# Bias rows at a pitch of 2 KB, longer assumed transfers in the list scheduler, and a new layout of the first transfers and products

## The chip, the core and the metric

The kernel runs on one core of one Trainium2 chip. The engines named here are TensorE (PE, its weight loads PEld), VectorE (DVE), ScalarE (ACT), GpSimd (POOL) and SyncE (SP, which issues nearly all transfers). The metric is the device time in microseconds (us), and less is better.

## What is computed

Two layers of an encoder over 768 tokens (512 of one request, 256 of another) with 1024 features, in float32. Layer 0 mixes tokens by windowed attention, layer 1 by a short convolution. The change lies in layer 0's mixer and in what is loaded for it:

```python
bias = rel_bias[t5_bucket(rel)]                      # 16 heads, 128 x 384 per query block
q, k, v = split(rms_norm(x, norm_mix[0]) @ w_qkv)    # 16 query heads, 4 key heads of 64
logits = q @ k.T * scale + bias, masked to +-128 tokens
p = softmax(logits with the sink)                    # out = p @ v, x = x + out @ w_o
...
x = x + (p[i] @ ple_w_proj[i]) * gate                # the product p[i] @ ple_w_proj[i] comes first
```

Every float32 operand of a product is split into a high and a low part (`hi`, `lo`), and three products stand for one: hi by hi, lo by hi, hi by lo.

## The kernel before

`mixer_attention` writes layer 0's mixer as a list of operations with costs. `Plan.order` is a list scheduler: it walks through them in a modelled time, engine by engine, and takes at each point the ready operation with the longest way to the end (`reach`). The order that comes out is what each engine's queue holds, in order. The modelled time of a transfer is its `lands` (bytes by 400 GB/s) behind a common pipe, 1.7 us after the issue, and 0.3 us more until it counts as landed (`done`, L549 and L550). The engines themselves run by semaphores, so the model only sets the order. SP, ACT and DVE each take their own queue strictly in order: an entry that waits holds up all entries behind it.

In that part of the program:

- **First products.** `p0` (two blocks of 128x768) and `w0` (128x1024) are loaded, split (L782 to L796), and multiplied for eight blocks m of 128 output rows, each in two pieces of 512 and 256 columns (`product`, L664, `halves`); `projected` copies the results to tiles `L` and stores them (`pj`). Ahead of them, PE runs matmuls on constants (`dummy`, tile `warm`, L755) and one product for the bias rows (`bp`, L762).
- **Inputs.** x is loaded in eight blocks (`x_in`), scaled and split to `xs` (L834, L837); squares are summed (L846, L848) for the norm, whose `rstd` reaches DVE late, at L878. Products by `w_k` and `w_q` need all of `xs`; their scaling (`kt`, `qt`) needs `rstd`.
- **Bias rows.** `brow` holds for each of 16 heads one row of 512 numbers. One transfer writes each row 32 times into DRAM (`skew`) with a pitch of SKEW numbers; 32 later transfers (`bias<-skew`, four to a tile, 16 to the first two head groups together) read it at a pitch of SKEW-1, so that each query's row is shifted by one.
- **Heads.** The halves of `kt` and `qt` that hold single heads are copied between partitions by transfers (`kk<-qh`, `kk<-ql`, `q<-qh`, `q<-ql`, 64 partitions each). Scores (`S`, L1052 and L1053) need q and k; the reduction behind them (L1059) needs the bias.
- **Values.** `values(n)` (`vp`, L980 to L982) multiplies xs by the three pieces of `w_v` (`wvh`, `wvl`); ACT and DVE empty its bank into `vv` (L995, L998). Tiles `wraw` are a ring of three buffers for loaded weights; a bank of PSUM with the tag mm1 exists once.

The layer's input p[1] is loaded to `wraw` and split within the same stage (`p`, L1180, L1183). After the attention stage the kernel leaves this scheduler; from there on its order is written out by hand.

Of the kernel before, what the change touches and what calls it, by code (L numbers as in the profile page):

```python
# [17 lines left out]
P = 128  # L18
# [9 lines left out]
CH = 1024  # L28

BM, BS, BO, BT, BL = 1, 3, 1, 2, 5  # L30

NA = 2
URGENT = 10.0

# [4 lines left out]

SKEW = 511  # L40
ROWS = 32
# [6 lines left out]
def trunk_kernel(ctx: ExitStack, tc: tile.TileContext, a: dict, out: bass.AP):  # L48
# [423 lines left out]
    class Plan:  # L472


        OWN = {"PE": 0.0, "ACT": 0.13, "DVE": 0.12, "POOL": 0.1, "SP": 0.0}
        OTHER = {"PE": 0.22, "ACT": 0.15, "DVE": 0.14, "POOL": 0.3, "SP": 0.1}
# [86 lines left out]
    def mixer_attention():  # L563
# [46 lines left out]
        def place(i, name, dt=F32R):  # L610
            return new(f"S{i}", 1, lambda: slot(i, name, dt))

        def dma(box, src, n, after=(), uses=(), queue="SP"):

            def run():
                d, s = src()
                (nc.sync if queue == "SP" else act).dma_start(d, s)

            lands = n / 400e3
# [33 lines left out]

        def product(ps, w, xs, o, n, col=0, ks=None, start=True, stop=True, prev=None):

            ks = range(len(xs)) if ks is None else ks
            for i, k in enumerate(ks):

                def run(i=i, k=k):
                    c = slice(col, col + P)  # L660
                    wh, wl = w.parts[0][k][:, c], w.parts[1][k][:, c]
                    xh, xl = (p[:, o : o + n] for p in xs[k].parts())
                    for j, (a_, b_) in enumerate(((wh, xh), (wh, xl), (wl, xh))):
                        pe.matmul(  # L664
                            ps.t[:, :n],
                            lhsT=a_,
                            rhs=b_,
                            start=start and i == 0 and j == 0,
                            stop=stop and i == len(ks) - 1 and j == 2,
                        )  # L670

                args = "PE", 3 * MM[n], run, [w.ready, xs[k].ready, prev], [ps.key, *w.keys, *xs[k].keys]
                if i == 0 and start:
                    prev = first(ps, *args[:3], args[3], args[4][1:])
                else:
                    prev = op(*args)
            return prev

        def halves(w, xs, tags, col=0):

            o, out = 0, []
            for tag, n in zip(tags, SEQS):
                ps = bank(tag)
                out.append((ps, o, n, product(ps, w, xs, o, n, col)))
                o += n
            return out
# [26 lines left out]
        def widen():  # L713
# [20 lines left out]
        table = op("ACT", 1.28, lambda: act.preload_act_table_set(EXP_LN), behind=[mk_in])  # L734
        got[1] = [dma(p0[1], lambda: (p0[1].t[:], a["p"][0, :, 1, :]), 393216)]
        w0.landed.append(
            dma(w0, lambda: (w0.t[:, 512:], a["proj"][0, 0, :, 512:]), 262144, uses=[w0.key])
        )
        w1 = fetched(a["proj"][0, 1])
        vec_in = dma(None, lambda: (vec[:], a["vec"][:]), 40960)  # L740
        x_in = []
        for m in range(KB):
# [3 lines left out]
            x_in.append(dma(b, lambda b=b, m=m: (b.t[:, m % 2, :], a["x"][m]), 393216, uses=[] if m % 2 == 0 else [b.key]))  # L746
        wk = fetched(a["w_k"][0])
        sink_in = dma(None, lambda: (sink[:], a["sink"][:].broadcast_to([P, HEADS])), 8192)
        for u, v in zip(DMAS := [got[0][0], w0.landed[0], got[1][0], w0.landed[1], w1.landed[0], vec_in, *x_in, wk.landed[0], sink_in], DMAS[1:]):
            v.behind.append(u)  # L750

        def dummy(n):
# [4 lines left out]

        d0 = first(warm, "PE", 3 * 0.45, dummy(3), [wide], [ones512.key])
        bp = bank("PT", "bp")
        bps = first(  # L760
            bp, "PE", 1.0,
            lambda: pe.matmul(bp.t[:HEADS, :], lhsT=rb.t[:], rhs=oh.t[:], start=True, stop=True),  # L762
            [rb_in, oh_in, d0], [rb.key, oh.key],
        )
# [10 lines left out]
        wt.keys, wt.ready = [wt.key], []  # L775
        part0 = []
        for k in range(2):
            c = slice(512 * k, 512 * k + 512)
            hi, lo = place(10 + k, "p0h"), place(12 + k, "p0l")

            def wh(c=c, k=k):
                act.activation(wt.t[0][:, c], w0.t[:, c], AF.Copy)  # L782
                wt.parts = [blocks(t[:], 2) for t in wt.t]

            def wl(c=c):
                dve.tensor_tensor(wt.t[1][:, c], w0.t[:, c], wt.t[0][:, c].bitcast(F32), ALU.subtract)

            if k == 0:
                h = first(wt, "ACT", A(512), wh, [w0.landed[0]], [w0.key])
                ph = first(hi, "DVE", 0.5, lambda hi=hi: dve.tensor_copy(hi.t[:], p0[0].t[:]), [got[0]], [p0[0].key])  # L790
            else:
                h = op("ACT", A(512), wh, [w0.landed[1]], [wt.key, w0.key])
                ph = first(hi, "ACT", A(T), lambda hi=hi: act.activation(hi.t[:], p0[1].t[:], AF.Copy), [got[1]], [p0[1].key])
# [4 lines left out]
            )  # L798
            l = op("DVE", V(512), wl, [h], [wt.key, w0.key])
            part0.append(block_of(hi, lo, [ph, pl, h, l]))  # L800
        w1 = prepared(w1, 2)
# [6 lines left out]
        def projected(l, m, w, part, t, tags, vector):  # L808
            ops = []
            for ps, o, n, last in halves(w, part, tags, m % 4 * P):  # L810

# [68 lines left out]
        rc = new("rc", 1, lambda: ap.tile([P, T // P], F32, name="rc", bufs=1))  # L880
        rt = bank("O", "rt")

# [3 lines left out]

        tr = first(rt, "PE", 0.4, columns, [rstd, d1], [r.key])
        rcs = first(rc, "DVE", 0.1, lambda: dve.tensor_copy(rc.t[:], rt.t[:, : T // P]), [tr], [rt.key])
# [22 lines left out]
        def keys(c, ps, tag):  # L911
            parts = scaled(ps, temp(tag, "kt"), False, tag)
            for j in range(2):
                g = 2 * c + j
                for kept, places, (part, ready) in ((khh, KHI, parts[0]), (kll, KLO, parts[1])):
                    dst = kept[g] = place(places[g], "kk")
                    dst.ready = []
                    for i in range(2):
# [6 lines left out]

                        dst.ready.append(dma(dst, ends, 196608, [ready], [part.key] + ([dst.key] if i else [])))

        def queries(c, w, tags, tag):
            parts = scaled(halves(w, xs, tags), temp(tag, "qt"), True, tag)
            for j in range(2):  # L930
# [3 lines left out]
                for i, (part, ready) in enumerate(parts):  # L934
# [6 lines left out]

                    dst.ready.append(dma(dst, ends, 196608, [ready], [part.key] + ([dst.key] if i else [])))

# [6 lines left out]
            ),  # L950
            1046528 * 4, [rowed], [brow.key],
        )
# [50 lines left out]
        for n in range(T // P):  # L1003
            values(n, ("O", "mm1")[n % 2] if n < 3 else "mm1")

# [1046 lines left out]
```

## Time and profile before

| | us |
|---|---|
| three runs, median (lowest, highest) | 1678.84 (1677.44, 1679.71) |
| the profiled execution, its own time | 1679.09 |
| its span in the trace | 1677.3 |

The page's second part cuts the span into 40 slices, with the busy share of each engine in tenths and the clock granted to TensorE (`PEclk`). A view by windows gives the same sums for stretches that one chooses. A view of waits names, for an engine, the instruction that stood idle and the last thing that released it. In a timeline a row holds start, duration, engine, line, operation, output and inputs, and in brackets the idle time ahead of it with its releaser. `SPq` rows are issues of transfers.

### The profile page before, as it was taken

How to read it: one execution, taken by the hardware profiler on the slowest of the kernel's cores; microseconds unless marked ns; L12 is line 12 of the kernel's file. 1: busy time of each engine (PE TensorE's matmuls, PEld its weight loads, DVE VectorE, ACT ScalarE, POOL GpSimd, SP SyncE). 2: the span in 40 equal slices, each digit the busy share in tenths (PEclk: the TensorE clock that was granted, in tenths of full speed). 3: DMA queues.
4: the chain of work that ended last, by engine and by line, in shares of the span. 5: the costliest groups of instructions: out<-in, count | busy, mean ns of one | idle time of the engine just before them, and what ended most of it. 6: DMA issues, size and time to landing. Idle time of an engine off the chain costs nothing. (4 is left out here: it accounts for less than half of the span.)

```text
span 1677.3 us, 24258 instructions
## 1 busy us (share of the span) xinstructions
PE 1641.3 (98%) x9428; PEld 1594.0 (95%) x9428; DVE 1394.3 (83%) x2215; ACT 919.9 (55%) x1454; POOL 13.5 (1%) x60
## 2 busy tenths in 40 slices
PE   9899899999999999999999999999999999999996
PEld 7788788999999999999999999999999999999986
DVE  6368598999899899886878877759989989998676
ACT  6269586765555555554655334545555545554554
POOL 0000000000000000000000000000000000000000
PEclk9899899999999999999999999999999999999998
DMA  9644432212222222122321221211122222222222
GB/s 265 165 113 139 107 95 91 97 50 72 76 73 67 76 76 76 64 95 66 111 82 51 76 76 63 89 63 51 64 76 76 70 69 76 76 67 85 79 89 98
DMA packets 47843, 144.59 MB, mean 86 GB/s; under 512 B 6080, under 2 KB 10688, under 8 KB 47728
## 3 DMA queue, kind: packets, MB, share of 16 engines
q1 hardware_dynamic: 47600, 142.94, 27.3%
q8 instruction: 74, 1.21, 0.3%
q14 instruction: 41, 0.34, 0.1%
q10 hardware_dynamic: 128, 0.10, 0.0%
HBM read 123.10 MB, written 10.48 MB: 80 GB/s over the span
## 5 line engine op out<-in xcount | busy, mean ns | idle before, releaser
L429 ACT ACTIVATE whi<-sum 128x1024 fp32r<-128x1024 f32 x66 | 70.1, 1062 | 257.8 <-PE a L461 221.8
L461 PE MATMUL a<-xs,whi 128*128 128x384 f32 x608 | 118.0, 335 | 0.7 <-DVE y L1549 0.6
L461 PEld LDWEIGHTS a<-xs,whi 128*128 128x128 f32 x608 | 106.4, 188 | 1.6 <-DVE y L1549 1.3
L461 PE MATMUL a<-t,whi 128*128 128x384 f32 x528 | 107.6, 336 | 0.0
L461 PE MATMUL b<-t,zhi 128*128 128x384 f32 x528 | 107.6, 336 | 0.0
L461 PE MATMUL a<-t,zhi 128*128 128x384 f32 x528 | 107.2, 336 | 0.0
L1585 DVE TENSOR_TENSOR x<-x,a 128x384 f32<-128x384 f32 x112 | 62.1, 554 | 53.7 <-PE a L461 53.6
L461 PE MATMUL a<-act,whi 128*128 128x384 f32 x448 | 96.1, 335 | 0.0
L461 PEld LDWEIGHTS a<-t,whi 128*128 128x128 f32 x528 | 93.4, 188 | 0.0
L461 PEld LDWEIGHTS b<-t,zhi 128*128 128x128 f32 x528 | 93.4, 188 | 0.0
L461 PEld LDWEIGHTS a<-t,zhi 128*128 128x128 f32 x528 | 93.3, 188 | 0.0
L429 ACT ACTIVATE zhi<-sum 128x1024 fp32r<-128x1024 f32 x66 | 69.8, 1057 | 36.9 <-DVE sum L405 31.2
L440 DVE TENSOR_TENSOR wlo<-wraw,whi 128x1024 fp32r<-128x1024 f32 x72 | 87.6, 1217 | 0.0
L429 ACT ACTIVATE whi<-wraw 128x1024 fp32r<-128x1024 f32 x72 | 75.6, 1050 | 19.4 <-issue 15.8
L664 PE MATMUL mm<-xs_mix,whi 128*128 128x512 f32 (+1 forms) x320 | 84.8, 354 | 0.2 <-ACT L L817 0.2
L440 DVE TENSOR_TENSOR zlo<-sum,zhi 128x1024 fp32r<-128x1024 f32 x66 | 80.4, 1218 | 0.5 <-ACT zhi L429 0.5
L440 DVE TENSOR_TENSOR wlo<-sum,whi 128x1024 fp32r<-128x1024 f32 x66 | 80.4, 1218 | 0.0
L461 PEld LDWEIGHTS a<-act,whi 128*128 128x128 f32 x448 | 79.4, 188 | 0.0
L461 PE MATMUL a<-xs,wlo 128*128 128x384 f32 x304 | 64.9, 334 | 0.0
L664 PEld LDWEIGHTS mm<-xs_mix,whi 128*128 128x128 f32 x320 | 57.3, 200 | 6.0 <-ACT L L817 0.4
L1059 DVE CUSTOM_DVE_ANT_0 L<-S,bias,nsink 128x256 f32<-128x256 f32 (+1 forms) x96 | 48.1, 522 | 16.9 <-issue 10.7
L1069 ACT ACTIVATE L<-L,mn 128x257 f32<-128x257 f32 (+1 forms) x96 | 51.5, 539 | 19.3 <-DVE mn L1059 19.2
(308 smaller groups left out, 4534.5 us busy)
## 6 DMA issues: line engine op xcount, KB each, us to landing
wraw<-in_up SPq DMA_DIRECT2D x64, 512.0 KB, 3.5
wraw<-in_down SPq DMA_DIRECT2D x64, 512.0 KB, 3.5
wraw<-in_w_in SPq DMA_DIRECT2D x24, 512.0 KB, 3.5
wraw<-in_gate SPq DMA_DIRECT2D x16, 512.0 KB, 3.5
wraw<-in_w_q SPq DMA_DIRECT2D x8, 512.0 KB, 6.2
wraw<-in_w_out SPq DMA_DIRECT2D x8, 512.0 KB, 3.5
x_in<-in_x SPq DMA_DIRECT2D x8, 384.0 KB, 6.7
pj<-L SPq DMA_DIRECT2D x8, 384.0 KB, 4.9
```

Source lines behind the costliest of these rows:

```text
L429: act.activation(hi[:], src, AF.Copy)
L440: dve.tensor_tensor(lo[:], src, hi[:].bitcast(F32), ALU.subtract)
L461: pe.matmul(ps, lhsT=a, rhs=b, start=start and i == 0, stop=i == len(terms) - 1, skip_group_check=True)
L664: pe.matmul(ps.t[:, :n], lhsT=a_, rhs=b_, start=start and i == 0 and j == 0, stop=stop and i == len(ks) - 1 and j == 2,)
L1059: dve.tensor_tensor_reduce(L.t[:, j, 1 : 1 + w], S.t[:, :w], bias[hp].t[:, j, j0 : j0 + w], 1.0, nsink[:, H_ : H_ + 1], ALU.add, ALU.min, ...
L1069: act.activation(L.t[:, j, : 1 + w], L.t[:, j, : 1 + w], AF.Exp, bias=mn.t[:, h : h + 1], scale=-1.0, accum_out=sm.t[:, h : h + 1])
L1585: dve.tensor_tensor(t[:, o : o + H], t[:, o : o + H], f, op)
```

## The change

The pitch of the bias rows becomes 512 numbers. The scheduler adds 6 us (`LATE`) to the way behind each transfer when it ranks operations, models the pipe with 1.3 us ahead and 1.2 us behind, takes 240 GB/s for the copies of q and k heads and 200 GB/s for the bias rows, whose bytes are no longer counted four times, and ranks the operations in a topological order. The first products become one operation for each matmul (`fine`), each waiting for the parts that it reads; w0 comes in three pieces, its first 128 columns ahead of everything; the bias table, the one-hot matrix and the mask move from ACT's queue to SP's, behind w_k; seven constant matmuls stand ahead of the first product in place of three and three; some banks change their tags.

```diff
-SKEW = 511
+SKEW = 512
+WARM = 7
...
+        LATE = 6.0
...
-            for o in reversed(self.ops):
-                tail = o.tail if o.tail is not None else self.OTHER[o.engine]
+            known, sorted_ = dict(after), [o for o in self.ops if after[id(o)] == 0]
+            for o in sorted_:
+                for n in nexts[id(o)]:
+                    known[id(n)] -= 1
+                    if known[id(n)] == 0:
+                        sorted_.append(n)
+            for o in reversed(sorted_):
+                tail = o.tail + self.LATE if o.tail is not None else self.OTHER[o.engine]
...
-                    pipe = max(pipe, t + o.cost + 1.7) + o.tail
-                    o.landed = pipe + 0.3
+                    pipe = max(pipe, t + o.cost + 1.3) + o.tail
+                    o.landed = pipe + 1.2
...
-            for i, k in enumerate(ks):
+            for k in range(len(xs)):
+                for js in ((0,), (1,), (2,)) if fine else ((0, 1, 2),):
...
+                    if fine:
+                        j = js[0]
+                        after = [wr[0], xs[k].ready[0], prev, (None, xs[k].ready[1], wr[1])[j]]
...
+        first_weights(slice(0, P))
         got[0] = [dma(p0[0], lambda: (p0[0].t[:], a["p"][0, :, 0, :]), 393216)]
-        w0.landed.append(dma(w0, lambda: (w0.t[:, :512], a["proj"][0, 0, :, :512]), 262144))
-        rb_in = dma(rb, lambda: (rb.t[:], a["rel_bias"][:]), 2048, queue="ACT")
-        oh_in = dma(oh, lambda: (oh.t[:], a["onehot"][:]), 65536, queue="ACT")
-        mk_in = dma(mk, lambda: (mk.t[:], a["mask"][:].broadcast_to([HEADS, 512])), 32768, queue="ACT")
+        first_weights(slice(P, 512))
         got[1] = [dma(p0[1], lambda: (p0[1].t[:], a["p"][0, :, 1, :]), 393216)]
+        first_weights(slice(512, CH))
...
-        d0 = first(warm, "PE", 3 * 0.45, dummy(3), [wide], [ones512.key])
-        bp = bank("PT", "bp")
+        d0 = first(warm, "PE", WARM * 0.48, dummy(WARM), [wide], [ones512.key])
+        bp = bank("O", "bp")
...
-            [rb_in, oh_in, d0], [rb.key, oh.key],
+            [rb_in, oh_in], [rb.key, oh.key],
...
-        d1 = op("PE", 3 * 0.3, dummy(3), [bps], [warm.key, ones512.key])
...
-        kps = halves(wk, xs, ("PT", "PT"))
+        kps = halves(wk, xs, ("O", "S"))
...
-                        dst.ready.append(dma(dst, ends, 196608, [ready], [part.key] + ([dst.key] if i else [])))
+                        dst.ready.append(dma(dst, ends, 196608, [ready], [part.key] + ([dst.key] if i else []), rate=240e3))
...
-            1046528 * 4, [rowed], [brow.key],
+            1048576, [rowed], [brow.key], rate=200e3,
...
-            values(n, ("O", "mm1")[n % 2] if n < 3 else "mm1")
+            values(n, "PT" if n < 3 else "mm1")
```

What the scheduler makes of it shows at three places. The first is PE's queue at the start of the program; `warm` is the constant matmul, `bp` the bias product, `mm` a first product, `p0h` and `p0l` the parts of its input. Before:

```order
L755 MATMUL warm<-warm,ones 128x512 x3
L762 MATMUL bp<-oh,rb 16x512
L755 MATMUL warm<-warm,ones 128x512 x3
L664 MATMUL mm<-p0h,whi 128x512
L664 MATMUL mm<-p0l,whi 128x512
L664 MATMUL mm<-p0h,wlo 128x512
```

And now:

```order
L774 MATMUL warm<-warm,ones 128x512 x7
L674 MATMUL mm<-p0h,whi 128x512
L674 MATMUL mm<-p0h,whi 128x256
L674 MATMUL mm<-p0h,whi 128x512 x2
L674 MATMUL mm<-p0h,whi 128x256
L674 MATMUL mm<-p0l,whi 128x512
L674 MATMUL mm<-p0h,wlo 128x512
```

The bias product has left this place (it now stands among the products by the second block of weights), and the hi parts are used for several outputs before the lo parts.

The second is SP's queue from the bias rows on; `skew<-brow` writes them, `bias<-skew` reads them, `wraw<-in_w_v` of 512 columns is the third piece of w_v. Before:

```order
L617 DMA skew<-brow 16x32x511
L617 DMA pj_86<-L 128x768
L617 DMA wraw<-in_w_v 128x768
L617 DMA pj_86<-L 128x768
L617 DMA bias<-skew 32x2x384 x10
L617 DMA wraw<-in_w_v 128x512
L617 DMA wraw<-in_w_q 128x1024
L617 DMA kk<-qh 64x768
```

And now:

```order
L625 DMA wraw<-in_w_v 128x768
L625 DMA pj_86<-L 128x768
L625 DMA skew<-brow 16x32x512
L625 DMA wraw<-in_w_v 128x512
L625 DMA wraw<-in_w_q 128x1024 x2
L625 DMA bias<-skew 32x2x384 x3
L625 DMA q<-qh 64x768 x2
L625 DMA bias<-skew 32x2x384
L625 DMA kk<-qh 64x768
```

The bias rows are written later, behind all stores of the first products; the third piece of w_v has moved from behind ten reads of them to ahead of all reads.

The third is ACT's queue where the second layer's input is split (`p_722`, now `p_727`) between emptyings of the value banks (`vv`). Before:

```order
L995 ACTIVATE vv<-vp,rc 128x4x64 x2
L1180 ACTIVATE p_722<-wraw 128x768
L995 ACTIVATE vv<-vp,rc 128x4x64
L642 ACTIVATE whi<-wraw 128x1024
L691 ACTIVATE qh<-qt 128x768
L995 ACTIVATE vv<-vp,rc 128x4x64
```

And now:

```order
L1021 ACTIVATE vv<-vp,rc 128x4x64 x2
L1206 ACTIVATE p_727<-wraw 128x768
L650 ACTIVATE whi<-wraw 128x1024
L1021 ACTIVATE vv<-vp,rc 128x4x64
L706 ACTIVATE qh<-qt 128x768
```

Two emptyings stand ahead of the split in both. Behind it stand, before, a third emptying whose bank PE's queue gives to the next product of values (`vp`), and now one whose bank goes to a product of q (`mm`, 256 columns).

More of the change, by code (lines that the diff above doesn't have):

```diff
@@ L611, in place, with dma @@
             return new(f"S{i}", 1, lambda: slot(i, name, dt))
-        def dma(box, src, n, after=(), uses=(), queue="SP"):
+        def dma(box, src, n, after=(), uses=(), queue="SP", rate=400e3):
             def run():
@@ L617, in run @@
                 (nc.sync if queue == "SP" else act).dma_start(d, s)
-            lands = n / 400e3
+            lands = n / rate
             if box is not None and box.op is None:
@@ L652, in prepared, with product, run @@
             return w
-        def product(ps, w, xs, o, n, col=0, ks=None, start=True, stop=True, prev=None):
-            ks = range(len(xs)) if ks is None else ks
-            for i, k in enumerate(ks):
[L659 to L676, printed above, removed]
+        def product(ps, w, xs, o, n, col=0, fine=False):
+            prev = None
+            for k in range(len(xs)):
+                for js in ((0,), (1,), (2,)) if fine else ((0, 1, 2),):
+                    def run(k=k, js=js):
+                        c = slice(col, col + P)
+                        wh, wl = w.parts[0][k][:, c], w.parts[1][k][:, c]
+                        xh, xl = (p[:, o : o + n] for p in xs[k].parts())
+                        for j in js:
+                            a_, b_ = ((wh, xh), (wh, xl), (wl, xh))[j]
+                            pe.matmul(
+                                ps.t[:, :n],
+                                lhsT=a_,
+                                rhs=b_,
+                                start=k == 0 and j == 0,
+                                stop=k == len(xs) - 1 and j == 2,
+                            )
+                    wr = w.ready(col // P, k) if callable(w.ready) else w.ready
+                    after = [wr, xs[k].ready, prev]
+                    if fine:
+                        j = js[0]
+                        after = [wr[0], xs[k].ready[0], prev, (None, xs[k].ready[1], wr[1])[j]]
+                    args = "PE", len(js) * MM[n], run, after
+                    if prev is None:
+                        prev = first(ps, *args, [*w.keys, *xs[k].keys])
+                    else:
+                        prev = op(*args, [ps.key, *w.keys, *xs[k].keys])
@@ L677, in product, with halves @@
             return prev
-        def halves(w, xs, tags, col=0):
+        def halves(w, xs, tags, col=0, fine=False):
             o, out = 0, []
@@ L683, in halves @@
                 ps = bank(tag)
-                out.append((ps, o, n, product(ps, w, xs, o, n, col)))
+                out.append((ps, o, n, product(ps, w, xs, o, n, col, fine)))
                 o += n
@@ L771, in mixer_attention, with wh @@
         turned = op("DVE", 0.1, lambda: dve.tensor_scalar(nsink[:], sink[:], -1.0, None, ALU.mult), [sink_in])
-        d1 = op("PE", 3 * 0.3, dummy(3), [bps], [warm.key, ones512.key])
         wt = pair_tiles()
-        wt.keys, wt.ready = [wt.key], []
+        wt.keys, wt.ready = [wt.key], lambda m, k: first_ready(m, k)
         part0 = []
[L777 to L781, printed above, removed]
+        parts = []
+        for n, c in enumerate((slice(0, P), slice(P, 512), slice(512, CH))):
+            def wh(c=c):
                 act.activation(wt.t[0][:, c], w0.t[:, c], AF.Copy)
@@ L786, in wl @@
                 dve.tensor_tensor(wt.t[1][:, c], w0.t[:, c], wt.t[0][:, c].bitcast(F32), ALU.subtract)
+            n = c.stop - c.start
+            if c.start == 0:
+                h = first(wt, "ACT", A(n), wh, [w0.landed[0]], [w0.key])
+            else:
+                h = op("ACT", A(n), wh, [w0.landed[1 + c.start // 512]], [wt.key, w0.key])
+            parts.append((h, op("DVE", V(n), wl, [h], [wt.key, w0.key])))
+        for k in range(2):
+            hi, lo = place(10 + k, "p0h"), place(12 + k, "p0l")
             if k == 0:
-                h = first(wt, "ACT", A(512), wh, [w0.landed[0]], [w0.key])
                 ph = first(hi, "DVE", 0.5, lambda hi=hi: dve.tensor_copy(hi.t[:], p0[0].t[:]), [got[0]], [p0[0].key])
             else:
-                h = op("ACT", A(512), wh, [w0.landed[1]], [wt.key, w0.key])
                 ph = first(hi, "ACT", A(T), lambda hi=hi: act.activation(hi.t[:], p0[1].t[:], AF.Copy), [got[1]], [p0[1].key])
@@ L798, in mixer_attention, with first_ready @@
             )
-            l = op("DVE", V(512), wl, [h], [wt.key, w0.key])
-            part0.append(block_of(hi, lo, [ph, pl, h, l]))
+            part0.append(block_of(hi, lo, [ph, pl]))
+        def first_ready(m, k):
+            return parts[2] if k else parts[0] if m == 0 else parts[1]
         w1 = prepared(w1, 2)
@@ L809, in projected @@
             ops = []
-            for ps, o, n, last in halves(w, part, tags, m % 4 * P):
+            for ps, o, n, last in halves(w, part, tags, m % 4 * P, l == 0):
                 def run(ps=ps, o=o, n=n):
@@ L880, in mixer_attention @@
         rc = new("rc", 1, lambda: ap.tile([P, T // P], F32, name="rc", bufs=1))
-        rt = bank("O", "rt")
+        rt = bank("PT", "rt")
         def columns():
@@ L885, in columns @@
                 pe.transpose(rt.t[:, n : n + 1], r.t[0:1, n * P : (n + 1) * P], ident[0:1, 0:1])
-        tr = first(rt, "PE", 0.4, columns, [rstd, d1], [r.key])
+        tr = first(rt, "PE", 0.4, columns, [rstd], [r.key])
         rcs = first(rc, "DVE", 0.1, lambda: dve.tensor_copy(rc.t[:], rt.t[:, : T // P]), [tr], [rt.key])
@@ L940, in ends @@
                         )
-                    dst.ready.append(dma(dst, ends, 196608, [ready], [part.key] + ([dst.key] if i else [])))
+                    dst.ready.append(dma(dst, ends, 196608, [ready], [part.key] + ([dst.key] if i else []), rate=240e3))
         wq = [prepared(fetched(a["w_q"][0]), KB)]
```

14 lines of the change are left out of this document (9 added, 5 removed).

## Prediction

> **What bounds the kernel now.** First the page: its head, the engines and the clock.
>
> ```profile
> span 1677.3 us, 24258 instructions
> PE 1641.3 (98%) x9428; PEld 1594.0 (95%) x9428; DVE 1394.3 (83%) x2215; ACT 919.9 (55%) x1454; POOL 13.5 (1%) x60
> PEclk9899899999999999999999999999999999999998
> ```
>
> PE is busy for 98% of the span, so a change can only win where PE stands idle or runs at a reduced clock. The page's clock row dips in slices 2 and 5, which is the stage that the change touches. A view by windows shows how much there is. Its columns are the stretch, its length, busy time with counts for PE, PEld, DVE, ACT and POOL, the granted clock, the DMA share and GB/s.
>
> ```profile
> 51.00:54.00 3.00, 0.47 (x2) 0.19 (x1) 0.61 (x1) 0.63 (x1) 0.00 (x0) 1.00 0.91 268
> 54.00:58.00 4.00, 3.86 (x16) 3.48 (x17) 1.71 (x3) 1.42 (x2) 0.00 (x0) 0.59 1.04 246
> 68.00:73.00 5.00, 0.34 (x2) 0.13 (x1) 1.35 (x2) 1.21 (x2) 0.00 (x0) 0.88 0.55 128
> 73.00:79.00 6.00, 6.00 (x23) 5.43 (x24) 0.00 (x0) 0.00 (x0) 0.00 (x0) 0.53 0.01 3
> 87.00:91.00 4.00, 1.53 (x9) 0.97 (x8) 0.69 (x1) 0.84 (x1) 0.00 (x0) 1.00 0.96 171
> 179.00:185.00 6.00, 6.00 (x22) 5.18 (x22) 2.19 (x6) 1.57 (x5) 0.37 (x2) 0.55 0.52 113
> 198.00:202.00 4.00, 4.00 (x14) 3.66 (x13) 3.34 (x13) 3.70 (x11) 0.00 (x0) 0.57 0.01 2
> 290.00:1660.00 1370.00, 1368.21 (x7844) 1357.85 (x7843) 1178.62 (x1703) 725.55 (x1025) 0.33 (x6) 1.00 0.23 75
> ```
>
> From 290 to 1660 us PE is idle for 1.8 us of 1370, and that order is written by hand and unchanged. Everything to be won lies ahead of 290 us. There PE's waits are these (line, releaser, total, times, longest):
>
> ```profile
> PE S L1052 <- DMA q<-ql: 4.9, 3, 2.5
> PE vp L980 <- DVE vv L998: 4.7, 1, 4.7
> PE S L1052 <- DMA bias<-skew: 3.3, 1, 3.3
> PE vp L980 <- ACT wvh L691: 2.3, 1, 2.3
> PE vp L981 <- DVE wvl L694: 0.3, 1, 0.3
> ```
>
> Four of them are followed by a stretch at about half clock, where PE is counted busy but does half the work. That adds 3.86 x 0.41 = 1.6 us behind the wait on w_v at 51, 6.00 x 0.47 = 2.8 behind the one at 68, 6.00 x 0.45 = 2.7 at 179 and 4.00 x 0.43 = 1.7 at 198. The wait that ends at 90 left the clock at 1.00. Waits and clock together cost 15.5 + 8.8 = 24 us, beside the start.
>
> **The change, term by term.** The sum is made against the profiled execution's 1679.1 us, of which 1677.3 are span; it lies 0.3 us over the median of the runs.
>
> *Start.* Timeline of the first product:
>
> ```profile
> 4.40 0.56 DVE L790 CAST p0h<-p 128x768 fp32r<-128x768 f32 x1 [2.70 <-DMA p<-in_p]
> 5.35 1.86 PE L762 MATMUL bp<-oh,rb 32*16 32x512 f32 x2 [1.94 <-DMA rb<-in_rel_bias]
> 7.14 1.65 PE L755 MATMUL warm<-warm,ones 128*128 128x512 f32 x3
> 8.59 0.63 PE L664 MATMUL mm<-p0h,whi 128*128 128x512 f32 x1
> 9.01 0.63 PE L664 MATMUL mm<-p0l,whi 128*128 128x512 f32 x1
> 10.57 0.39 PE L664 MATMUL mm<-p0h,wlo 128*128 128x512 f32 x1
> 10.80 0.39 PE L664 MATMUL mm<-p0h,whi 128*128 128x512 f32 x1
> ```
>
> The input is split from 4.40 on, yet the first product starts at 8.59, since the bias product and three constant matmuls stand ahead of it. Now neither does. The input still lands near 4.4, because the 64 KB of w0 put ahead of it replace the 98 KB that ACT's queue sent beside it; with one more issue ahead I take 4.4 to 4.9. The first product can start at about 5.5, 3 us earlier. Not all of that stays. A matmul of 512 columns takes 0.42 us there (8.59 to 9.01), and 0.23 once the clock is up (10.57 to 10.80). By 10.3 the kernel before has done 4 of them, 0.9 us of full-clock work. At half clock from 5.5 on the new one does 4.8/0.42 x 0.23 = 2.6; with the clock up from 7 it is held by what has arrived, some 4.5. From either goes 0.9 for the bias product, two matmuls in 1.86 us at half clock, which PE must now do among the products. That leaves a gain of 0.8 to 2.7; I take 1.5. From there DVE sets the pace of the loads' splitting, with nearly the same work.
>
> The Trainium skill (TensorE: Matmul & The Clock Gate, What's actually happening) says that a free-running window of about 3.4 us of sustained work raises the clock. By it the seven constant matmuls, 3.0 us at half clock, do not fill a window alone, so the phase decides and the sum keeps both ends of this term; the trace agrees so far, as three did not raise it.
>
> *The third piece of w_v (wait at 51).* The rows of the SP and ACT queues, and the transfers:
>
> ```profile
> 27.21 0.42 SPq L617 DMA_DIRECT2D skew<-brow  x1
> 33.20 4.66 SPq L617 DMA_DIRECT2D pj<-L  x1
> 42.46 0.79 SPq L617 DMA_DIRECT2D bias<-skew  x2
> 52.73 0.63 ACT L691 ACTIVATE wvh<-wraw 128x512 fp32r<-128x512 f32 x1 [5.97 <-DMA wraw<-in_w_v]
> skew<-brow SPq DMA_DIRECT2D x1, 1022.0 KB, 15.2
> 30.00:40.00 10.00, 10.00 (x57) 8.64 (x56) 7.29 (x9) 5.45 (x9) 1.78 (x2) 1.00 0.94 99
> 8.00:11.00 3.00, 3.00 (x9) 2.32 (x9) 2.41 (x3) 2.38 (x4) 0.00 (x0) 1.00 1.03 398
> ```
>
> SP stood at the first read of the bias rows until they had landed at 42.4, then issued ten reads, and only then the last piece of w_v, which landed at 52.7. In the new order that piece goes out ahead of all reads. What remains is the transfer of the rows itself, since it is issued later (behind the last store of the first products, which SP reached by 33; I take 32.5) and the piece travels behind it. Whether 4 more bytes for each row change its rate the trace does not show. It moved 99 GB/s with the DMA engines 94% busy, where loads move 398. The ends are 2.6 us for 1.05 MB at the second rate, and 10.5 at the first; a rate below the first is a rival below. The nearest row is the transfer itself, so I take 10.5 and its 15.2 us to landing: 47.7, the piece 0.5 later, its split 0.63, ready at 48.9. PE's queue holds 42.7 us of matmul work ahead of the first use before, reached at 51.1, and 40.8 now (each matmul at the pitches shown). So PE arrives at 51.1 - 1.9 - 1.5 = 47.7 and waits 1.2, too short to lower the clock. Before: 2.3 + 0.3 + 1.6 = 4.2. Gain 3.0.
>
> *The input behind the value banks (wait at 68).*
>
> ```profile
> 62.52 0.33 SPq L617 DMA_DIRECT2D wraw<-in_p  x1
> 70.59 0.84 ACT L1180 ACTIVATE p<-wraw 128x768 fp32r<-128x768 f32 x1 [8.56 <-DMA wraw<-in_p]
> 71.34 0.46 ACT L995 ACTIVATE vv<-vp,rc 128x256 fp32r<-128x256 f32 x1
> 72.34 0.48 DVE L998 SCALAR_TENSOR_TENSOR vv<-vp,rc,vv 128x256 fp32r<-128x256 f32 x1
> ```
>
> ACT and DVE stood at the split of p until its load landed; the emptying of a value bank behind it came too late for PE. The same split still stands ahead of an emptying. But the bank is wanted after 62.0 us of PE work in place of 55.0; DVE has 2.3 us more to do between (two scalings, one split), so the load may come 4.7 us of PE work later, as much as the whole wait. Besides, 2 copies of q and 7 reads of the bias fewer go out ahead of it; at the 0.33 us that its own issue takes, that is 3 us earlier. I take the wait as gone, with its clock: 4.7 + 2.8 = 7.5.
>
> *The copies of q (waits at 88, 175, 194).* In all three the scores wait for copies of q; the one at 175 is put down to bias rows, but copies issued up to 172 are in front of those.
>
> ```profile
> 170.38 0.41 SPq L617 DMA_DIRECT2D xa<-in_x  x1
> 170.87 1.11 SPq L617 DMA_DIRECT2D q<-ql  x2
> 58.49 0.28 PE L980 MATMUL vp<-wvh,xs_mix 128*128 128x256 f32 x1
> 58.60 0.28 PE L981 MATMUL vp<-wvl,xs_mix 128*128 128x256 f32 x1
> ```
>
> Counted in the orders, between the last product of such a q and its first score stand 18, 21 and 21 matmuls of 512 columns before and 21, 21 and 31 now, with 28, 20 and 21 of 256 columns before and 40, 29 and 12 now, and transposes at 0.09 us. At 0.23 and 0.12 us that is 7.5, 8.3 and 7.4 us of cover before, and 9.6, 9.4 and 9.0 now. The waits of 2.5, 3.3 and 2.2 shrink to 0.4, 2.2 and 0.6, and the second loses some 1.3 more because the load of x (384 KB, at 300 GB/s or so by the windows) no longer goes out ahead of the copies. A fourth q gets a shorter lead, 10.7, which still is more than the 7.4 + 2.2 = 9.6 needed at 194. Gains: 2.1, then 2.4 with 2.7 of clock, then 1.6 with 1.7: 10.5.
>
> *Sum.* 1.5 + 3.0 + 7.5 + 10.5 = 22.5. Against it I set 2.5 for new small waits, about as much as all short waits before 290 us come to, since the same work of DVE must fit into less time:
>
> ```profile
> 83.00:275.00 192.00, 183.02 (x1106) 160.08 (x1105) 152.58 (x420) 143.97 (x355) 8.98 (x43) 0.97 0.39 106
> ```
>
> DVE's 152.6 us in 192 become 152.6 in 181.5, 84%. **1679.1 - 20 = 1659 us.** The planner's numbers themselves cost nothing; constants in a model are not executed.
>
> **Rivals.** *The pitch makes the rows fast.* At 2.6 to 5 us the third piece of w_v is there in time and its 1.2 us go, with 0.3 or so on copies behind the reads: 1657.5. For it speaks that 99 GB/s is far under other transfers; against it, that the source is the same 16 partitions, each read 32 times. The Trainium skill (SBUF — State Buffer, Door 1: The DMA port swizzle) has a port for each group of partitions at 27.2 GB/s; partitions 0 to 15 reach four, 109 GB/s whatever the pitch. The trace's 99 agrees, and by it this rival falls and 1659 stays.
>
> *The waits on q stay.* If the copies land as much later as the scores do, because reads of the bias and q now crowd together, or if DVE paces the scores, the 10.5 are not won: 1669.5. For it: the copies are 64 partitions in a shared queue. Against it: in the stretch from 83 to 275 the DMA share is 0.39.
>
> *Slower.* The rows' transfer stands ahead of the third piece of w_v, and of w_q, in the same queue. Should the pitch of 2048 bytes slow it, PE waits for all of it from 47.7 on. The point from which this eats the 20 us is a transfer 20 us longer, 31 us in place of 10.5, 34 GB/s. At four times the time it is 42 us, and the kernel takes 1659 + 31 = 1690. [...] Against it: loads with rows of 4 KB move 398 GB/s.
>
> **How the numbers follow.** The forecast, 1659, has 0.50; the fast rows 0.20; the waits on q 0.18; nothing won, because as much is lost in waits that I do not see, 0.04; slower 0.08. The first three hold 0.88 and lie between 1657.5 and 1669.5. The start's ends add 1.2 down and 0.7 up, and no new small waits another 2.5 down. The range is 1652 to 1670. Three runs of this kernel differ by 0.13%, so about 0.2% (3.4 us) is what can be told from no change: faster 0.88, same 0.04, slower 0.08.
>
> **What would show it.** Right: the first product near 5.5; no wait over 1.5 us at the third piece of w_v; no wait of the value banks on DVE; the split of p standing before PE needs it; waits on q under 1.5 us each, and a granted clock of 1.00 in every window from 12 to 290 us. Wrong: a transfer of the rows clearly shorter or longer than 10.5 us, a wait of PE over 2 us ahead of 290 us, or DVE over 95% busy with PE idle beside it. The span from the attention stage's end on should be as before; if it moved, the change reaches further than I read.

## The result, and the profile after

The changed kernel takes 1655.36 us (median; 1653.76 to 1657.81, four runs), the kernel before 1678.14 beside it: a ratio of 0.9864, interval 0.9847 to 0.9881. The forecast was 1659 us with a range of 1652 to 1670. The profiled execution took 1654.76 us, 24.3 less than the one before.

The head of the page and its clock row:

```profile
span 1653.0 us, 24266 instructions
PE 1631.7 (99%) x9429; PEld 1587.2 (96%) x9429; DVE 1393.4 (84%) x2216; ACT 918.4 (56%) x1455; POOL 10.7 (1%) x60
PEclk9999999999999999999999999999999999999998
```

DVE and ACT do the same work as before in 24 us less, and the clock row has lost its two dips. The same stretches as before, by windows (length, busy time of PE, PEld, DVE, ACT and POOL, granted clock, DMA share, GB/s):

```profile
51.00:54.00 3.00, 3.00 (x26) 2.90 (x25) 0.00 (x0) 0.31 (x1) 0.00 (x0) 1.00 0.94 265
54.00:58.00 4.00, 4.00 (x25) 3.52 (x24) 0.48 (x1) 0.17 (x1) 0.00 (x0) 1.00 1.04 219
68.00:73.00 5.00, 5.00 (x37) 4.68 (x36) 3.77 (x8) 1.94 (x5) 0.00 (x0) 1.00 0.83 236
73.00:79.00 6.00, 5.64 (x32) 4.59 (x31) 3.59 (x8) 3.48 (x6) 0.00 (x0) 1.00 0.94 246
87.00:91.00 4.00, 4.00 (x29) 3.82 (x28) 0.63 (x2) 1.42 (x4) 0.00 (x0) 1.00 0.00 0
179.00:185.00 6.00, 6.00 (x40) 5.23 (x39) 5.91 (x16) 5.95 (x15) 0.37 (x2) 1.00 0.00 0
198.00:202.00 4.00, 4.00 (x30) 3.62 (x29) 3.94 (x15) 2.10 (x8) 0.37 (x2) 1.00 0.99 236
83.00:275.00 192.00, 190.01 (x1173) 168.74 (x1173) 160.37 (x422) 147.95 (x354) 8.87 (x43) 1.00 0.39 106
```

PE runs at full clock in each of them and stands idle in only one of the short ones, for 0.4 us between 73 and 79. The stretch from 83 to 275 held 183.02 us of busy PE and now holds 190.01 (its last 12 us lie behind the stage now). What PE still waits for ahead of 290 us, by 0.3 us or more (line, releaser, total, times, longest):

```profile
PE warm L774 <- DVE warm L729: 1.8, 1, 1.8
PE S L1078 <- DMA bias<-skew: 1.3, 1, 1.3
PE vp L1006 <- DVE vv L1024: 1.1, 1, 1.1
PE mm L130 <- DVE xa L1189: 0.6, 1, 0.6
PE S L1078 <- DMA q<-ql: 0.4, 1, 0.4
PE vp L1007 <- DVE wvl L709: 0.3, 1, 0.3
```

One row of the windows shows how far this accounts for the result, the first of the kernel before and the second of the changed one:

```profile
0.00:290.00 290.00, 269.13 (x1566) 233.23 (x1567) 206.07 (x492) 188.72 (x417) 13.16 (x54) 0.96 0.50 138
```

```profile
0.00:290.00 290.00, 283.95 (x1710) 251.19 (x1711) 224.98 (x525) 201.59 (x439) 10.40 (x54) 1.00 0.51 144
```

PE's idle time falls from 20.9 to 6.1 us, which is 14.8. The half-clock stretches that the prediction added up to 8.8 us are gone. Together that is 23.6 of the 24.3 us. Behind the wait at the stage's end PE goes on at 263.1 us in place of 287.8, so the whole gain lies ahead of that place; what follows takes 1389.9 us in place of 1389.5.

### The profile page after: what moved, and what is told of

Its sections match the earlier page's. It is cut to its first block, busy times and chain, and to the rows that moved or that the text cites. A ratio compares the mean times of both kernels' runs of the same rounds, so it can differ in the third digit from the quotient of the medians.

```text
span 1653.0 us, 24266 instructions
## 1 busy us (share of the span) xinstructions
PE 1631.7 (99%) x9429; PEld 1587.2 (96%) x9429; DVE 1393.4 (84%) x2216; ACT 918.4 (56%) x1455; POOL 10.7 (1%) x60
## 5 line engine op out<-in xcount | busy, mean ns | idle before, releaser
L430 ACT ACTIVATE zhi<-sum 128x1024 fp32r<-128x1024 f32 x66 | 69.8, 1057 | 37.0 <-DVE sum L406 31.3
L674 PE MATMUL mm<-xs_mix,whi 128*128 128x512 f32 (+1 forms) x320 | 81.2, 340 | 0.0
L462 PE MATMUL b<-t,zlo 128*128 128x384 f32 x264 | 61.1, 335 | 0.8 <-DVE zlo L441 0.8
L462 PE MATMUL a<-t,zlo 128*128 128x384 f32 x264 | 61.1, 335 | 0.0
L462 PE MATMUL a<-t,wlo 128*128 128x384 f32 x264 | 60.9, 334 | 0.0
```

The costliest lines, as they stand in the source:

```text
L430: act.activation(hi[:], src, AF.Copy)
L462: pe.matmul(ps, lhsT=a, rhs=b, start=start and i == 0, stop=i == len(terms) - 1, skip_group_check=True)
L674: pe.matmul(ps.t[:, :n], lhsT=a_, rhs=b_, start=k == 0 and j == 0, stop=k == len(xs) - 1 and j == 2,)
```

## The experiments

In the tables, "behind its work" is the time at which PE reaches a place less the matmul work that its order puts ahead of that place, priced at full clock as in the prediction (the constant matmuls count as work). What it grows by between two places was lost there.

### The pitch alone: e1_pitch511

```diff
-SKEW = 512
+SKEW = 511
```

> The changed kernel with the pitch of the bias rows back at 511 numbers; the order of every queue is the changed kernel's. My theory: the pitch is worth nothing, the rows still move at about 100 GB/s for 10 us and land some 13.4 us after the issue at 31.7; the time stays within 1.5 us of 1655.4. Rival (rows of 2 KB are what lets the third piece of w_v come in time): the rows take 2 us or more longer, PE waits 2 to 4 us for the third piece of w_v near 47 and the clock may drop behind it: 1658 to 1662.

It took 1656.20 us (ratio to the kernel before 0.9863, 0.9844 to 0.9882), the same as the changed kernel. A window in the middle of the rows' transfer, at a pitch of 511 and, in the changed kernel, of 512:

```profile
37.00:45.00 8.00, 7.76 (x53) 6.81 (x52) 5.70 (x10) 3.75 (x6) 0.07 (x1) 1.00 0.92 98
```

```profile
36.00:43.00 7.00, 6.92 (x49) 6.21 (x47) 4.77 (x8) 3.37 (x5) 0.00 (x0) 1.00 0.90 97
```

98 and 97 GB/s: the pitch that gives the change its name is worth nothing that these runs can show.

### The start without the numbers, the numbers without the start: e2_start_only, e3_numbers_only

e2 is the changed kernel with the scheduler's old numbers:

```diff
-SKEW = 512
+SKEW = 511
-        LATE = 6.0
+        LATE = 0.0
-                    pipe = max(pipe, t + o.cost + 1.3) + o.tail
-                    o.landed = pipe + 1.2
+                    pipe = max(pipe, t + o.cost + 1.7) + o.tail
+                    o.landed = pipe + 0.3
-            1048576, [rowed], [brow.key], rate=200e3,
+            1046528 * 4, [rowed], [brow.key],
...
```

The lines left out drop `rate=240e3` twice. e3 puts exactly these numbers, and the topological ranking, into the kernel before. Both have that ranking, so neither shows what it is worth, and e2 does not part the new start from the banks' new tags.

> The changed kernel with all of the scheduler's numbers as before (LATE 0, the old pipe, 400 GB/s for every transfer, the bias rows counted four times) and pitch 511: only the new start, the banks' tags and the topological order are left. In this order the cover of the three q is 7.6, 8.4 and 7.5 us of PE work, as before. My theory (the numbers carry the gain, the start 0.8 to 2.7 us): the waits on q near 85, 170 and 190 are still there, with half clock behind one or two of them; 1679 - 2.5 - up to 3 for a changed wait at w_v: 1671 to 1678. Rival (the start carries most of the gain): 1658 to 1665.

> The kernel before with the scheduler's numbers of the change alone (LATE 6, the new pipe, the rates, topological ranking); start, banks and pitch 511 as before. Cover of the three q: 9.7, 9.5 and 9.1 us. My theory: the waits on q shrink to under 1.5 us each and the clock stays up (10.5 us), the wait at 68 on the value banks goes (7.5 us); the third piece of w_v stands behind five reads of the bias rows in place of ten and keeps a wait of 1 to 2 us: 1659 to 1664. Rival (each part helps little alone, since PE's waits only move): over 1668.

e2 took 1672.77 us (0.9963, 0.9952 to 0.9975), e3 1662.37 (0.9901, 0.9882 to 0.9920): 6 and 17 us less than the kernel before. Each time lies where it was expected, the way there only in part:

| us behind its work | first product of x | bank of rstd (`rt`) | first score | wait at the stage's end |
|---|---|---|---|---|
| before | 7.5 | 7.6 | 20.6 | at 287.8 |
| e2, start alone | 4.2 | 8.7 | 10.4 | at 281.0 |
| e3, numbers alone | 7.7 | 12.6 | 15.6 | at 271.0 |
| changed | 4.8 | 5.0 | 7.8 | at 263.1 |

In e2 the start gains 3.3 us and gives 4.5 back by `rt`. Windows of e2:

```profile
28.00:30.00 2.00, 1.55 (x6) 1.29 (x7) 2.00 (x4) 2.00 (x5) 0.00 (x0) 0.87 0.30 61
30.00:33.00 3.00, 3.00 (x12) 2.63 (x11) 2.90 (x4) 0.99 (x2) 0.00 (x0) 0.52 0.98 357
```

DVE and ACT are both full while PE waits for them, and half clock follows. With the new numbers the same start keeps its gain. In e3 the wait for the third piece of w_v is gone, but another has come:

```profile
PE rt L892 <- DVE rstd_mix L885: 4.6, 1, 4.6
```

and on e3's ACT, from the timeline:

```profile
43.59 0.85 ACT L698 ACTIVATE wvh<-wraw 128x768 fp32r<-128x768 f32 x1 [6.36 <-DMA wraw<-in_w_v]
44.34 1.03 ACT L878 ACTIVATE ln<-ss,eps 128x512 f32<-128x512 f32 x2
```

A piece of w_v travelled beside the slow bias rows, its split stood ahead of the norm's logarithm, and `rstd` came late. The slow transfer still cost 4.6 us, now through ACT. The two parts add up (6 + 17 = 23), but only in the sum: neither removes a fixed set of waits.

### The numbers taken apart: e4_late0, e7_rates_old

e4 sets LATE to 0, e7 takes back the rates:

```diff
-        LATE = 6.0
+        LATE = 0.0
```

```diff
-dst.ready.append(dma(dst, ends, 196608, [ready], [part.key] + ([dst.key] if i else []), rate=240e3))
+dst.ready.append(dma(dst, ends, 196608, [ready], [part.key] + ([dst.key] if i else [])))
-            1048576, [rowed], [brow.key], rate=200e3,
+            1046528 * 4, [rowed], [brow.key],
```

> The changed kernel with LATE at 0; pipe, rates, start and pitch as changed. The third piece of w_v stands again behind ten reads of the bias rows and two copies of k; the covers of q are 8.6, 9.7 and 9.2 us. My theory: the wait for w_v is back (2 to 4 us, half clock behind it 1.6), the first q loses 1 us: 1660 to 1665. Rival (LATE does nothing that the rates don't do, or PE has enough work in hand): 1654 to 1657. Rival (LATE carries the whole gain): 1670 to 1676.

> The changed kernel with the old rates in the model (400 GB/s for the copies of q and k, the bias rows counted four times); LATE, pipe and start as changed. Cover of the three q: 9.7, 8.1 and 7.7 us, of the fourth 9.9. My theory (a q needs 10.0, 11 and 9.6 us from its last product to its first score, and what the cover lacks PE waits): waits of 0.3, 2.5 to 3.4 and 1.9 us, with half clock behind at least one of them, 1.5 to 2.7: 1659 to 1662. Rival (the copies come sooner when they are issued sooner, so the wait doesn't follow the cover): 1655 to 1657.

e4 took 1666.66 us (0.9925, 0.9898 to 0.9952), 1.7 over what I expected. The order was read rightly: on SP's queue the third piece of w_v stands behind the reads,

```profile
45.09 5.40 SPq L625 DMA_DIRECT2D bias<-skew  x10
50.59 1.17 SPq L625 DMA_DIRECT2D kk<-qh  x2
51.86 0.53 SPq L625 DMA_DIRECT2D wraw<-in_w_v  x1
```

and PE waits 2.3 us for it, as before the change. What I had left out is that e4 also loses 4.7 us between the first product of x and `rt`, as e2 does, and waits 1.5 us for a fourth q. e7 took 1661.49 us (0.9901, 0.9881 to 0.9921), inside what was expected, but in the main for another reason. Waits of PE in e7, and a window behind the first of them:

```profile
PE S L1078 <- DVE qt L923: 3.8, 1, 3.8
PE S L1078 <- DMA q<-ql: 2.8, 2, 1.7
71.00:74.00 3.00, 2.89 (x13) 2.89 (x14) 3.00 (x6) 0.84 (x1) 0.00 (x0) 0.50 0.32 77
```

The waits on q came to 1.7 and 1.1 us, below the 2.5 to 3.4 and 1.9 expected. The 3.8 us are the input's (see e10 below): its load went out at 60.6 here. With the half clock behind them, 2.89 x 0.50 = 1.4 us, they come to 5.2, about all that this profiled execution takes more than the changed kernel's (5.1).

The two sides of "what the cover lacks, PE waits" (cover in us of PE work, counted in each order, plus the wait that the trace shows):

| | first q | second q | third q |
|---|---|---|---|
| before | 7.5 + 2.5 = 10.0 | 8.3 + 3.3 = 11.6 | 7.4 + 2.2 = 9.6 |
| e2, start alone | 7.6 + 3.1 = 10.7 | 8.4 + 3.1 = 11.5 | 7.5 + 2.1 = 9.6 |
| e4, LATE 0 | 8.6 + 1.7 = 10.3 | 9.7 + 1.8 = 11.5 | 9.2 + 0.4 = 9.6 |
| e7, old rates | 9.7, no wait | 8.1 + 1.7 = 9.8 | 7.7 + 1.1 = 8.8 |
| changed | 9.6 + 0.4 = 10.0 | 9.4 + 1.3 = 10.7 | 9.0, no wait |
| e1, pitch 511 | 9.6, no wait | 9.4 + 1.2 = 10.6 | 9.0 + 1.6 = 10.6 |

The cover went from 7.4 to 9.7 us, and the need stayed between 8.8 and 11.6. The last two rows, one order twice, show how far it moves from one execution to the next.

### The constant matmuls: e5_warm0

```diff
-WARM = 7
+WARM = 0
```

> The changed kernel with no constant matmuls (WARM 0); all else as changed. The first product then starts near 4.9 with a clock that has seen no work. My theory (the constant matmuls fill the time in which the clock must see work, so the clock comes up one window of 3.4 us later without them): the 0.23 us pitch begins near 8.5 to 10.3 in place of 5.8 to 7.0, and the kernel loses half of that, 1 to 2 us: 1656.5 to 1657.5. Rival (the products alone raise the clock as soon, or what is lost at half clock is waited for later anyway because DVE sets the pace of the splitting): 1655 to 1656.

1656.82 us (1656.69 to 1659.46; 0.9874, 0.9857 to 0.9891). The ranges overlap, so the time does not decide it. PE's timeline of e5, then of the changed kernel:

```profile
6.97 0.63 PE L674 MATMUL mm<-p0l,whi 128*128 128x512 f32 x1
7.39 0.63 PE L674 MATMUL mm<-p0h,wlo 128*128 128x512 f32 x1
```

```profile
5.11 1.90 PE L674 MATMUL mm<-p0h,whi 128*128 128x512 f32 x5
6.85 0.40 PE L674 MATMUL mm<-p0l,whi 128*128 128x512 f32 x1
7.08 0.39 PE L674 MATMUL mm<-p0h,wlo 128*128 128x512 f32 x1
```

From 6.97 to 7.39 a matmul takes 0.42 us without the constants; from 6.85 to 7.08 it takes 0.23 with them. In the seven profiles with the changed start and seven constant matmuls (changed, e1, e6 to e10) the pitch of 0.23 begins between 5.5 and 6.9 us, in e5 at 9.5. They do bring the clock up earlier. What this is worth drowns in something else: in five of the seven (changed, e1, e7, e8, e10) PE reached the first product of x between 21.3 and 22.5 us, in e6 and e9, whose bias product is another, at 21.4 and 23.7, and in e5 at 22.3.

### The bias rows on all partitions: e6_rows_spread

```diff
-pe.matmul(bp.t[:HEADS, :], lhsT=rb.t[:], rhs=oh.t[:], ...)
+nc.gpsimd.tensor_copy(rb8[:]..., rb.t[:, :, None].broadcast_to([32, HEADS, 8]))
+pe.matmul(bp.t[:], lhsT=rb8[:], rhs=oh.t[:], ...)
-skew = dram.tile([HEADS, (ROWS + 1) * SKEW], ...)
+skew = dram.tile([HEADS, (ROWS + 8) * SKEW], ...)
-brow.t[:HEADS, None, :SKEW].broadcast_to([HEADS, ROWS, SKEW])
+brow.t[:, None, :SKEW].broadcast_to([P, ROWS // 8 + 1, SKEW])
...
```

The lines left out load the mask to 128 partitions and let DVE make `brow` on as many.

> The changed kernel with each bias row standing on eight partitions (the bias product gives 128 rows in place of 16) and written from all 128 partitions, five times each with 25 percent more bytes, at the same pitch of 512; order as changed. My theory (the 98 GB/s are set by the 16 partitions that are read, not by the pitch): the rows move at 250 GB/s or more, 1.31 MB in at most 5.3 us, and land 6 us or more earlier; the waits of 0.3 and 1.1 us around the third piece of w_v go, which is all that hangs on it: 1653.5 to 1655.5. Rival (the writes of 2 KB rows to memory set the rate): 13 us at 98 GB/s, the third piece of w_v 3 us later, 1657 to 1660.

1652.73 us (0.9844, 0.9830 to 0.9859), 0.8 under what I expected. The rows' transfer in e6 (issues, KB, us from issue to landing; it went out at 32.4), and a window in the middle of it:

```profile
skew<-brow SPq DMA_DIRECT2D x1, 1280.0 KB, 7.7
36.00:39.00 3.00, 3.00 (x21) 2.70 (x20) 1.49 (x3) 2.53 (x5) 0.19 (x1) 1.00 1.05 383
```

The changed kernel's own row:

```profile
skew<-brow SPq DMA_DIRECT2D x1, 1024.0 KB, 13.4
```

A quarter more bytes at the same pitch land in 7.7 us, at 383 GB/s in place of 97 in the middle. So neither the pitch nor the writing of rows of 2 KB sets the rate; reading them from 16 partitions does. (Each partition is also read five times in place of 32, which this run does not part from their number.) The Trainium skill (SBUF — State Buffer, Door 1: The DMA port swizzle) has the number of partitions: it measured 104 GB/s for a transfer of 1 MiB on partitions 0 to 15 and 328 on all 128. The 97 here is near the first; the 383, which leaves out the ends of the transfer, is above the second. PE's waits of 0.3 and 1.1 us around the third piece of w_v are gone in e6.

### A lower rate for the copies: e8_copies_160, and both: e9_spread_and_160

```diff
-dst.ready.append(dma(dst, ends, 196608, [ready], [part.key] + ([dst.key] if i else []), rate=240e3))
+dst.ready.append(dma(dst, ends, 196608, [ready], [part.key] + ([dst.key] if i else []), rate=160e3))
```

> The changed kernel with 160 GB/s in place of 240 assumed for the copies of q and k. Cover of the three q: 12.2, 10.0 and 11.7 us, of the fourth 15.7. My theory: no wait on the first, third and fourth, 0.6 to 1.5 us on the second: 1654 to 1655.5. Rival (the longer cover takes work from elsewhere, and a wait of the values or of the score banks comes in its place): over 1656.5.

> The changed kernel with both of the last edits: rows of the bias on 128 partitions and 160 GB/s assumed for the copies of q and k. My theory (the two take away different waits: 1.5 us around the third piece of w_v, 1.5 us on q): PE's waits ahead of 290 us come down to the start, the 0.6 us at the stage's end and some tenths, 1650.5 to 1652. Rival (the earlier rows already took the q waits' place, or PE's queue then waits for DVE): 1652.5 to 1654.

e8 took 1653.89 us (0.9852, 0.9837 to 0.9866), which these runs can't tell from the changed kernel; the waits on q left are 0.16 and 0.35 us. e9 took 1650.93 us (1650.41 to 1653.72, five runs; 0.9837, 0.9822 to 0.9853). Its median is the lowest here, and each of its runs is below each of the changed kernel's, though the intervals of the ratios overlap a little; from e6 (1651.55 to 1653.81) these runs can't tell it. Its waits:

```profile
PE warm L774 <- DVE warm L729: 1.8, 1, 1.8
PE bp L783 <- POOL rb L782: 1.4, 1, 1.4
PE mm L674 <- ACT whi L805: 0.7, 1, 0.7
PE mm L130 <- DVE xa L1195: 0.6, 1, 0.6
PE vp L1012 <- DVE qt L929: 0.2, 1, 0.2
```

From 24 to 260 us no wait over 0.2 us is left; what remains is the start and the 0.6 us at the stage's end. The start was dear in this execution. The wait of 1.4 us for the bias product ended at 20.3, and the clock fell behind it:

```profile
21.00:24.00 3.00, 3.00 (x12) 2.31 (x12) 2.87 (x5) 3.00 (x5) 0.00 (x0) 0.72 1.03 413
24.00:27.00 3.00, 3.00 (x13) 2.59 (x13) 3.00 (x4) 2.76 (x4) 0.00 (x0) 0.71 0.94 366
```

That is 3.00 x 0.28 + 3.00 x 0.29 = 1.7 us more. The profiled execution took 1653.22 us, one of the two longer ones of five (1653.22 and 1653.72; the others 1650.41 to 1650.93).

### The input's load put back in time: e10_input_later

```diff
+                ordered = plan.order()
+                at = ordered.index(moved[0])
+                sps = [i for i in range(at + 1, len(ordered)) if ordered[i].engine == "SP"]
+                ordered.insert(sps[5] + 1, ordered[at])
+                del ordered[at]
-                for o in plan.order():
+                for o in ordered:
```

`moved[0]` is the load of the second layer's input, first half.

> The changed kernel with one entry moved on SP's queue: the load of the second layer's input goes out behind two copies of q and four reads of the bias, near 62 us in place of 57.4, which is the time at which it went out before the change. My theory (that the bank is wanted 7 us of PE work later is what removed the wait at 68, and there is under 1 us of room left): the load lands near 68 to 70, the bank is emptied 4.3 us behind that, PE wants it at 69.8 and waits 2.5 to 5 us with half clock behind it: 1658 to 1663. Rival (the crowded queue, not the issue, sets when it lands): within 1 us of 1655.4.

1658.34 us (1657.67 to 1658.75; 0.9878, 0.9864 to 0.9892): 3 us more, at the lower edge. Timelines around the split, of the changed kernel (ACT, then DVE) and of e10 (ACT, then PE):

```profile
65.20 0.85 ACT L1206 ACTIVATE p<-wraw 128x768 fp32r<-128x768 f32 x1 [11.03 <-DMA wraw<-in_p]
...
69.02 0.48 DVE L1024 SCALAR_TENSOR_TENSOR vv<-vp,rc,vv 128x256 fp32r<-128x256 f32 x1
```

```profile
69.28 0.84 ACT L1210 ACTIVATE p<-wraw 128x768 fp32r<-128x768 f32 x1 [14.31 <-DMA wraw<-in_p]
...
71.77 0.38 PE L1078 MATMUL S<-kk,q 128*128 128x256 f32 x1 [2.33 <-DVE qt L923]
```

The load lands 4.1 us later and PE loses 2.6, at full clock: 2.3 before the second score, 0.3 before the bank that I had named. The scaling of q, which frees the second score's bank, stands on DVE between the split and that emptying, so it is late first. In e7 the same load, 3.4 us later than in the changed kernel, cost 3.8 us at this place, with half clock behind it.

## Why the prediction was right

**What bounds it.** Right: the gain lies ahead of the stage's end, and all but 0.7 us of it is PE's idle time and the half clock that was counted.

**Start (taken 1.5, ends 0.8 and 2.7).** The first product was forecast near 5.5 and came at 5.11, the full clock by 6.85. PE reaches the first product of x 4.8 us behind its work in place of 7.5. That is 2.7, or 2.5 without the seventh constant matmul, which counts as work: near the upper end. In the other four profiles with the same start (e1, e7, e8, e10) the figure lies between 5.1 and 5.9, a gain of 1.4 to 2.2, so 1.5 was as good a value as the trace allowed. The seven constants did not raise the clock before the products began, as said (from 5.11 to 6.85 the products still run at half clock); e5 shows that they help to raise it soon after.

**Third piece of w_v (taken 3.0).** SP's rows of the changed kernel:

```profile
31.67 0.49 SPq L625 DMA_DIRECT2D skew<-brow  x1
32.27 0.94 SPq L625 DMA_DIRECT2D wraw<-in_w_v  x1
35.64 7.03 SPq L625 DMA_DIRECT2D wraw<-in_w_q  x2
45.05 1.28 SPq L625 DMA_DIRECT2D bias<-skew  x3
```

The rows landed 13.4 us after an issue at 31.7, against 15.2 after 32.5 in the sum. So the wait is 0.3 in place of 1.2, and its clock stays up: 3.9 gained. That 1.2 us would have been too short to lower the clock is not shown: in e9 a wait of 1.4 us was followed by a lower clock.

**Input behind the value banks (taken 7.5).** The wait of 4.7 us and its 2.8 us of clock are gone. The forecast gave two reasons. By the first, the load may come 4.7 us later in PE's work, because the bank is wanted later; that alone was to cover the whole wait. It did not take in that PE, with its other waits gone, arrives earlier itself (at the first score 7.8 us behind its work in place of 20.6). The bank's emptying ends at 69.5 us and PE wants it at 69.8, so the room is 0.3 us. By the second, the load goes out 3 us earlier; it went out 5.1 earlier, at 57.4 in place of 62.5. Both were needed: e10, with the load out at 63.6, loses 2.6 us, and e7, with the load out at 60.6, 3.8 and 1.4 of clock. So the term came out right with little room, and in part by luck; the runs do not divide it between the two reasons.

**Copies of q (taken 10.5).** Forecast remainders 0.4, 0.9 (2.2 less 1.3) and 0.6; measured 0.4, 1.3 and none, at full clock. The waits were 2.5, 3.3 and 2.2 with 4.4 us of clock, so 10.7 are gained. That they fit so closely is partly chance: with nearly the same order the three waits came to 1.1 us in e6, 2.7 in e10 and 2.9 in e1, against 1.6 here and 1.9 in the forecast. The 1.3 us put down to the load of x were not tested by themselves.

**New small waits (set against it, 2.5).** The term that was too large. One new wait stands out, 1.1 us for `vv` at 50.5. ACT's row and DVE's two rows ahead of it:

```profile
47.77 1.06 ACT L650 ACTIVATE whi<-wraw 128x1024 fp32r<-128x1024 f32 x1 [0.65 <-DMA wraw<-in_w_q]
48.86 1.23 DVE L654 TENSOR_TENSOR wlo<-wraw,whi 128x1024 fp32r<-128x1024 f32 x1 [0.75 <-ACT whi L650]
50.00 0.48 DVE L1024 SCALAR_TENSOR_TENSOR vv<-vp,rc,vv 128x256 fp32r<-128x256 f32 x1
```

It does not come from a full DVE, as the forecast supposed: the emptying stood behind the split of w_q, whose load came behind the slow rows. In e6, where the rows land sooner, it is gone. Counted with the rows' transfer, the term of w_v gives 2.8 in place of 3.9. DVE is at 160.4 us of 192 in the stretch from 83 to 275, 84% as computed, and no wait on it follows there. With the start (1.0), w_v (0.9), the copies of q (0.2) and this (1.4) the forecast gain of 20 becomes 23.5; the 0.8 us left of 24.3 stay open.

**Rivals and signs.** The fast rows fell: 97 and 98 GB/s at the two pitches, and e6 shows that reading from 16 partitions holds them there. The waits on q went. A slow transfer did not come. One of the forecast's signs failed: a wait of the value banks on DVE is there, the 1.1 us above. The others that were looked for held: no wait over 2 us ahead of 290, a granted clock of 1.00 in the stretches shown, and the time behind the stage as before. The range's lower end, 1652, lies under what its own terms give (1657.5 - 1.2 - 2.5 = 1653.8); the measured time is above both.

## What to carry to other kernels

This list scheduler's model did not need true transfer times: ranking the operations as if each transfer came 6 us later, with the other new numbers, put loads and copies ahead of work and gave 17 us (e3). Taken out of the changed kernel one at a time, the 6 us cost 11 us (e4) and the rates 6 (e7). Count for each copy the work that covers it and add the wait seen; if the sum is the same in several orders, the cover is what to change. And when a transfer runs at a quarter of the others' rate, look at how many partitions it touches before its pitch.

## What the runs showed of the hardware

A wait of 2.5 us at 88 in the kernel before left the clock up, while behind the waits of 2.3 us at 51 and 2.2 us at 194 it stood at 0.59 and 0.57 for 4 us; in e10 2.3 us left it up, and in e9 it fell behind one of 1.4 us. The length alone does not decide. The Trainium skill (TensorE: Matmul & The Clock Gate, What's actually happening) has a window that runs free of the program. Such a window would explain these rows; no run here shows it by itself. The same section has the clock fall after an idle window of about 3.4 us, and here far shorter waits lowered it.

The same first instructions also differ from one execution to the next: with one start, that of e6 and e9, PE reached the first product of x at 21.4 and 23.7 us, more than half as wide as the spread of the changed kernel's runs (4 us).
